# Where a normalised activation starts in SBUF, and how its columns are cut into matmuls, in a fused decoder layer

## The chip, the cores and the metric

The kernel runs on one core of one Trainium2 chip. The metric is the time of one execution on the device in microseconds, the median of several runs. Before the change it is 2046.19 us (three runs, 2044.81 to 2046.81).

## What is computed

One decoder layer with 16 learned meta tokens ahead of 512 positions (L = 528), model width 2048. The first part of the reference is what the change touches:

```python
n = _rmsnorm(h, g_mix[l])
p = n @ w_in[l]
q, k, v, gb, gc, u = jnp.split(p, np.cumsum([...]), axis=-1)
q = _rmsnorm(q.reshape(b, L, N_ATTN_HEADS, HEAD_DIM), g_q[l])
k = _rmsnorm(k.reshape(b, L, N_ATTN_HEADS, HEAD_DIM), g_k[l])
...
o_conv = gb * _causal_dwconv(gc * u, conv_w[l])
```

q, k and v have 8 heads of 128; b, c and u (gb, gc and u above) have 1024 channels. Behind it come the stick-breaking attention, a norm of each group, one output projection with residual, and a SwiGLU feed-forward network (FFN, width 5632) with residual. The meta positions are dropped at the end, so q and b are needed for 512 positions only (META = 16 to L), k and v for all 528.

## The kernel before

Everything is held transposed: channels on the 128 partitions, positions along the free dimension. Products keep float32 accuracy by splitting each operand into a rounded high part and a remainder (type fp32r, 4 bytes) and summing three matmuls: high x high, high x low, low x high (`product_steps`, L311 to L313). The weights arrive by DMA in pieces of 8 k tiles (128 x 1024), ACT writes the high part (L202) and DVE the remainder (L203) into `sw_split`, three buffers deep.

**Normalised x.** `n_tiles` (L353) are 16 tiles, one for each 128 channels, with two rows per partition: row 0 holds the high part (written by ACT, L383), row 1 the low part (DVE, L384). A row is L + 48 floats = 2304 bytes (9 x 256) and a tile 4608 bytes (18 x 256), so all 32 rows start at the same place modulo 256 bytes. In the built program tile n0 starts at byte 104,096 of a partition, which is 160 modulo 256. The data starts 40 floats (160 bytes) into the row, so position 0 lies at 64 modulo 256, position 16 at 128, position 256 at 64.

**The products on n.** Each `product` walks two weight pieces of 8 k tiles. Within a piece it goes over the parts of the output, and within a part over the 8 k tiles, three matmuls each. The parts before the change:

- k and v of each head, 528 positions (`parts_of_all`, L398): 256 positions into the end of one PSUM bank and then 272 into the start of the next. The two lie side by side, and `flat` (L395) reads them as one row of 528.
- q of each head (L416, L530) and the first two b tiles, pb0 and pb1 (L710, L758): 512 positions in one matmul into one bank.
- pc0 and pu0 (L684): two parts of 258 positions from position 14 (C0) on.

The first head's k and q are made together while x arrives (L419 to L433). In the other heads the order is k, q, v. Between matmuls `tick` (L293) calls work that was put off by a number of k tiles (`after`, L290): the norms of k and q, and of the head before, the transposes of v and the scores z (`attend`, L544), the cumulative sums (`sums`, L613) and the weighted sum (`mix`, L643). With one part, `tick` comes after each k tile; with two, after every second step of a part. What TensorE executes is the order that the tile scheduler writes out from this.

**The conv stage.** Pairs of c and u tiles (`conv_pair`, L828, 258 columns) and later of b tiles (`gate_pair`, L840, 256 columns) use a seven-product scheme (`pair_product`, L797, matmuls at L793 to L795). Four of its seven blocks read n itself: `raw_block` from position 14 or 270 (16 or 272 in the gate pairs) and `last_block` (L743), a part of n that eight DMAs (L765) overwrite with mixed data once pb1 has been read; the other three read `mixed` tiles.

**The FFN.** It uses the same `pair_product`, 256 columns at a time, on tiles made by `slots` (L884). There the data starts 4 floats into a tile whose start is 224 modulo 256 bytes, so each operand starts at 240 modulo 256, and all lengths are multiples of 1024 bytes.

The weight operands start at 128 modulo 256 bytes everywhere.

Of the kernel before, what the change touches and what calls it, by code (L numbers as in the profile page):

```python
# [22 lines left out]
KT = D // P  # L23
# [3 lines left out]
T2 = SEQ // 2  # L27
# [6 lines left out]
def hybrid_layer(ctx: ExitStack, tc: tile.TileContext, xT, w_in, w_out, w_gu, w_down, vecs, out):  # L34
# [18 lines left out]
    npool = open_pool("npool", side="right")  # L53
# [21 lines left out]
    g_q, g_k = vec[:, 48:49], vec[:, 49:50]  # L75
# [24 lines left out]
    gq_s = const.tile([P, 1], F32, name="gq_s")  # L100
# [174 lines left out]
    def next_w():  # L275
        ahead = max(min(n_first, used[0] + 6), used[0] + 1 + S_AHEAD)
        if used[0] < n_first:
            ahead = min(ahead, n_first + 1)
        while len(split_w) < min(len(pieces), ahead):
            if n_first < len(split_w) <= n_first + S_AHEAD:  # L280
                with tc.issue_after(read_q0[3].ins):
                    prepare()
            else:
                prepare()
        used[0] += 1
        return split_w[used[0] - 1]
# [3 lines left out]
    def after(k_tiles, work):  # L290
        waiting.append([k_tiles, work])

    def tick():  # L293
        for w in waiting:
            w[0] -= 1
        while any(w[0] <= 0 for w in waiting):
            w = next(w for w in waiting if w[0] <= 0)
            waiting.remove(w)
            w[1]()

    def product_steps(parts, acts, n):

        k, last = 0, n - 1
        while k <= last:

            hi, lo = next_w()
            ws = [(hi[:, a : a + P], lo[:, a : a + P]) for a in range(0, hi.shape[-1], P)]
            for n_part, (ps, a, b) in enumerate(parts):
                for i, (wh, wl) in enumerate(ws):
                    ah, al = acts[k + i]  # L310
                    pe.matmul(ps, wh, ah[:, a:b], start=k + i == 0, stop=False)  # L311
                    pe.matmul(ps, wh, al[:, a:b], start=False, stop=False)  # L312
                    pe.matmul(ps, wl, ah[:, a:b], start=False, stop=k + i == last)  # L313
                    if (n_part * len(ws) + i + 1) % len(parts) == 0:
                        tick()
            k += len(ws)
            yield

    def product(parts, acts):
        for _ in product_steps(parts, acts, len(acts)):  # L320
            pass
# [28 lines left out]


    H = L // 2
    n_tiles = [npool.tile([P, 2, L + 48], F32R, name=f"n{k}")[:, :, 40:] for k in range(KT)]  # L353
    n_parts = [[t[:, part] for part in range(2)] for t in n_tiles]
    npool.tile([P, 52], F32, name="pad_n")
    n_hl = []
# [3 lines left out]
    ms, r, eps_r2, r2 = accs[1], rpool.tile([P, L], F32, name="r"), accs[1], acc  # L360
# [32 lines left out]
            ve.tensor_tensor(accs[k % 2], accs[k % 2], s, ALU.add)  # L393

    def flat(ps):  # L395
        return ps.rearrange("p a b -> p (a b)")[:, T2 : T2 + L]

    def parts_of_all(ps):  # L398
        return [(ps[:, 0, T2:], 0, T2), (ps[:, 1, : L - T2], T2, L)]

    def two(t):
        return t.rearrange("p (a b) -> p a b", a=2)
# [1 line left out]
    def read_qk(ps, g, cols):  # L404

        raw = t512(L, "e", 2)[:, :cols]
        s = t512(L, "e2", 2)[:, :cols]
        sc.activation(s, ps, AF.Square)
        last = sc.activation(raw, ps, AF.Copy, scale=g)
        return raw, s, cols, last  # L410

    pk0 = pp.tile([P, 2, 512], F32, tag="pp", name="pk0")
    pq0 = pp.tile([P, 2, 512], F32, tag="pp", name="pq0")
    steps = [
        product_steps(parts_of_all(pk0), n_hl, KT),
        product_steps([(pq0[:, 0, :], META, L)], n_hl, KT),  # L416
    ]

    for a, b in FIRST:  # L419
# [9 lines left out]
    for a, b in FIRST:  # L429
        for k in range(a, b):  # L430
            split_x(k)
        for step in steps:
            next(step)  # L433
    read_k0, read_q0 = read_qk(flat(pk0), g_k, L), read_qk(pq0[:, 0, :], gq_s, SEQ)
    for k in range(6):
        square_x(k)
    with tc.issue_after(read_k0[3].ins):
# [29 lines left out]
    def load_mix(k):  # L467
        xs[k] = xpool2.tile([P, 4, N], F32, tag="x", name=f"x_mix{k}")
        for m in range(4):
            at = C0 + m % 2 * T2  # L470
            tc.keep_in_program_order(nc.sync.dma_start(xs[k][:, m], xT[k + m // 2 * 8][:, at : at + N]))
# [16 lines left out]
    def qk_norm(read, dst, parts_of, name, then=None):  # L488

        raw, s, cols = read[:3]  # L490
        sh = apool.tile([P, L], F32R, tag="sh", name=f"sh_{name}")[:, :cols]
        sl = apool.tile([P, L], F32R, tag="sl", name=f"sl_{name}")[:, :cols]
        cuts = [(0, cols)] if cols == SEQ else [(0, T2), (T2, L)]
        split(sh, sl, s)

        def finish():
            v = t512(L, "v", 2)[:, :cols]
            for a, b in cuts:
                q = small(f"ss_{name}{a}")[:, : b - a]
                pe.matmul(q, ones_r, sh[:, a:b], start=True, stop=False)  # L500
                pe.matmul(q, ones_r, sl[:, a:b], start=False, stop=True)
                ve.scalar_tensor_tensor(
                    v[:, a:b], q, 1.0 / P, eps_r2[:, L - cols + a : L - cols + b], ALU.mult, ALU.add
                )
            rsqrt(dst, v, cols, times=raw)
            hi, lo, n = parts_of
            last = split(hi, lo, dst[:, :n])
            if then:
                with tc.issue_after(last[0].ins), tc.issue_after(last[1].ins):
                    then()  # L510

        return finish
# [3 lines left out]
    def head(h):  # L516

        if h:
            pk = pp.tile([P, 2, 512], F32, tag="pp", name=f"pk{h}")
            product(parts_of_all(pk), n_hl)  # L520
        read = read_qk(flat(pk), g_k, L) if h else read_k0
        kn = kns[0]
        kh = apool.tile([P, 384], F32R, tag="kh", name=f"kh{h}")
        kl = apool.tile([P, 384], F32R, tag="kl", name=f"kl{h}")
        after(8 if h else 19, qk_norm(read, kn[:, :L], (kh, kl, 384), f"k{h}"))

        if h:
            load_mix(h - 1)
            pq = pp.tile([P, 2, 512], F32, tag="pp", name=f"pq{h}")
            product([(pq[:, 0, :], META, L)], n_hl)  # L530
        read = read_qk(pq[:, 0, :], gq_s, SEQ) if h else read_q0
        qn = apool.tile([P, SEQ], F32, tag="qn", name=f"qn{h}")
        qh = apool.tile([P, SEQ], F32R, tag="qh", name=f"qh{h}")
        ql = apool.tile([P, SEQ], F32R, tag="ql", name=f"ql{h}")
        after(9 if h else 22, qk_norm(read, qn, (qh, ql, SEQ), f"q{h}", (lambda: mix_x(h - 1)) if h else None))

        pv = pp.tile([P, 2, 512], F32, tag="pp", name=f"pv{h}")
        product(parts_of_all(pv), n_hl)
        vt = t512(L, "e", 2)
        with tc.high_priority(0 if h else 1 << 20):  # L540
            ve.tensor_tensor(vt[:, :L], flat(pv), r, ALU.mult)
        after(6 if h else 15, lambda: attend(h, kn, kh, kl, qn, qh, ql, vt))
# [119 lines left out]
    for h in range(HEADS):  # L662
        head(h)
# [43 lines left out]
    y0 = t512(L, "e2", 2)[:, :SEQ]  # L707
    conv3(y0, cu0, 0)
    pb = pp.tile([P, 2, 512], F32, tag="pp", name="pb0")
    product([(pb[:, 0, :], META, L)], n_hl)  # L710
    gb0 = t512(L, "v", 2)[:, :SEQ]
    ve.tensor_tensor(gb0, pb[:, 0, :], r[:, META:], ALU.mult)
    assert not waiting
    apool.release()
    xpool2.release()
# [3 lines left out]
    def oc_slot(i, dt, name):  # L719
        return ocpool.tile([P, SEQ], dt, tag=f"oc{i}", name=name)  # L720
# [34 lines left out]
    CN = SEQ + 2  # L755
    gb1 = oc_slot(7, F32, "gb1")
    pb = pp.tile([P, 2, 512], F32, tag="pp", name="pb1")
    product([(pb[:, 0, :], META, L)], n_hl)  # L758
    ve.tensor_tensor(gb1, pb[:, 0, :], r[:, META:], ALU.mult)
    sm.release()  # L760
    pp.release()
    xyz = open_pool("xyz", 2, space=PSUM)
# [166 lines left out]
    for i, j in enumerate(OUT_TILES):  # L929
# [34 lines left out]
        ps = ps_out[i]  # L964
        half, k = divmod(j, 8)
# [266 lines left out]
```

## Time and profile before

| | |
|---|---|
| median of three runs | 2046.19 us (2044.81 to 2046.81) |
| the profiled execution | 2046.62 us, span 2044.8 us |
| granted TensorE clock | 0.999 of full |
| head stage (first product to the end of v of the last head) | about 6 to 343 us |
| pc0, pu0, pb0, pb1 | 343 to 395 us |
| conv stage | 395 to 600 us |
| output projection | 600 to 774 us |
| FFN | 774 to 2044 us |

TensorE appears as PE (matmuls) and PEld (weight loads), VectorE as DVE, ScalarE as ACT, GpSimd as POOL, SyncE as SP. [...]

A row of the table of windows gives the stretch in us, its length, then for each engine the busy time and the number of instructions, then the granted clock, the busy share of the DMA engines and GB/s. A row of the groups gives line, engine, operation, tiles, shape and count, then busy time and mean ns, then the idle time ahead and what ended it. A row of the timeline gives start, duration, engine, line, operation, tiles and shape, and in brackets a wait ahead of it.

### The profile page before, as it was taken

How to read it: one execution, taken by the hardware profiler on the slowest of the kernel's cores; microseconds unless marked ns; L12 is line 12 of the kernel's file. 1: busy time of each engine (PE TensorE's matmuls, PEld its weight loads, DVE VectorE, ACT ScalarE, POOL GpSimd, SP SyncE). 2: the span in 40 equal slices, each digit the busy share in tenths (PEclk: the TensorE clock that was granted, in tenths of full speed). 3: DMA queues.
4: the chain of work that ended last, by engine and by line, in shares of the span. 5: the costliest groups of instructions: out<-in, count | busy, mean ns of one | idle time of the engine just before them, and what ended most of it. 6: DMA issues, size and time to landing. Idle time of an engine off the chain costs nothing.

```text
span 2044.8 us, 39586 instructions
## 1 busy us (share of the span) xinstructions
PE 2027.8 (99%) x16134; PEld 1962.6 (96%) x16134; DVE 1728.4 (85%) x2187; ACT 1074.9 (53%) x1555; POOL 349.3 (17%) x514
## 2 busy tenths in 40 slices
PE   9999999999999999999999999999999999999999
PEld 8899999899998888999999999999999999999999
DVE  7877677698887778998988988988988978888887
ACT  7766667444454435555555554555555544444443
POOL 0111112200004441011111111111111242131211
PEclk9999999999999999999999999999999999999999
DMA  6343334732355555456465465455455899797764
GB/s 220 105 134 117 122 114 152 268 119 94 114 191 176 172 162 194 142 176 182 138 176 169 133 174 171 136 172 167 141 175 161 271 342 349 171 314 199 214 154 90
DMA packets 156086, 356.28 MB, mean 174 GB/s; under 512 B 13632, under 2 KB 67648, under 8 KB 155136
## 3 DMA queue, kind: packets, MB, share of 16 engines
q1 hardware_dynamic: 72208, 216.76, 32.6%
q0 software_dynamic: 83696, 136.99, 25.0%
q8 instruction: 126, 2.06, 0.4%
q14 instruction: 56, 0.46, 0.1%
HBM read 275.78 MB, written 77.92 MB: 173 GB/s over the span
## 4 chain that ended last, share of the span: by engine, by line
PE 89%; DVE 4%; ACT 2%; DMA 2%; issue 1%; POOL 1%; SPq 0%; DVEq 0%; ACTq 0%
PE x L793 13%; PE x L795 13%; PE x L794 13%; PE z L794 6%; PE z L795 6%; PE z L793 6%; PE y L795 3%; PE y L793 3%; PE y L794 3%; DVE sw_split L203 2%; PE pv L311 1%; PE pv L312 1%; PE pv L313 1%; PE pq L313 1%; PE pq L312 1%
## 5 line engine op out<-in xcount | busy, mean ns | idle before, releaser
L202 ACT CAST sw_split<-sw_in 128x1024 fp32r<-128x1024 f32 (+2 forms) x668 | 661.5, 992 | 712.1 <-PE z L794 189.0
L203 DVE TENSOR_TENSOR sw_split<-sw_in,sw_split 128x1024 fp32r<-128x1024 f32 (+2 forms) x668 | 778.0, 1165 | 150.2 <-ACT sw_split L202 144.7
L793 PE MATMUL x<-f,sw_split 128*128 128x256 f32 x1408 | 388.3, 276 | 2.9 <-ACT sides L813 1.9
L795 PE MATMUL x<-f,sw_split 128*128 128x256 f32 x1408 | 388.2, 276 | 0.6 <-DVE sw_split L203 0.6
L794 PE MATMUL x<-f,sw_split 128*128 128x256 f32 x1408 | 388.1, 276 | 0.0
L793 PEld LDWEIGHTS x<-f,sw_split 128*128 128x128 f32 x1408 | 265.0, 188 | 3.3 <-ACT sides L813 2.1
L795 PEld LDWEIGHTS x<-f,sw_split 128*128 128x128 f32 x1408 | 265.1, 188 | 1.0 <-DVE sw_split L203 1.0
L794 PEld LDWEIGHTS x<-f,sw_split 128*128 128x128 f32 x1408 | 265.1, 188 | 0.0
L1047 POOL DMA_DIRECT2D fd<-s x147 | 103.7, 922 | 713.7 <-DVE s L324 713.0
L209 DVE TENSOR_TENSOR sw_in<-sw_in 128x1024 f32<-128x1024 f32 (+1 forms) x164 | 187.9, 1146 | 11.5 <-DMA sw_in<-w_in 3.0
L793 PE MATMUL z<-f,sw_split 128*128 128x256 f32 x704 | 193.7, 275 | 0.3 <-ACT sides L815 0.3
L794 PE MATMUL z<-f,sw_split 128*128 128x256 f32 x704 | 193.6, 275 | 0.0
L795 PE MATMUL z<-f,sw_split 128*128 128x256 f32 x704 | 193.6, 275 | 0.0
L795 PE MATMUL x<-ring,sw_split 128*128 128x256 f32 x608 | 167.3, 275 | 0.4 <-DVE sw_split L203 0.4
L793 PE MATMUL x<-ring,sw_split 128*128 128x256 f32 x608 | 167.2, 275 | 0.0
L794 PE MATMUL x<-ring,sw_split 128*128 128x256 f32 x608 | 167.2, 275 | 0.0
L793 PEld LDWEIGHTS z<-f,sw_split 128*128 128x128 f32 x704 | 132.2, 188 | 0.5 <-ACT sides L815 0.5
L794 PEld LDWEIGHTS z<-f,sw_split 128*128 128x128 f32 x704 | 132.2, 188 | 0.0
L795 PEld LDWEIGHTS z<-f,sw_split 128*128 128x128 f32 x704 | 132.2, 188 | 0.0
L795 PEld LDWEIGHTS x<-ring,sw_split 128*128 128x128 f32 x608 | 114.1, 188 | 0.6 <-DVE sw_split L203 0.6
L794 PEld LDWEIGHTS x<-ring,sw_split 128*128 128x128 f32 x608 | 114.1, 188 | 0.0
L793 PEld LDWEIGHTS x<-ring,sw_split 128*128 128x128 f32 x608 | 114.1, 188 | 0.0
(604 smaller groups left out, 5459.2 us busy)
## 6 DMA issues: line engine op xcount, KB each, us to landing
sw_in<-w_gu SPq DMA_DIRECT2D x176, 512.0 KB, 3.9
sw_in<-w_in SPq DMA_DIRECT2D x92, 512.0 KB, 3.3
fd<-s POOLq DMA_DIRECT2D x147, 256.0 KB, 5.3
sw_in<-w_down SPq DMA_DIRECT2D x96, 384.0 KB, 4.2
ring<-fd POOLq DMA_DIRECT2D x42, 768.0 KB, 16.8
sw_in<-w_out SPq DMA_DIRECT2D x32, 512.0 KB, 3.4
out_T<-d POOLq DMA_DIRECT2D x54, 256.0 KB, 5.2
mix_dram<-st_x POOLq DMA_DIRECT2D x16, 516.0 KB, 4.0
```

Source lines behind the costliest of these rows:

```text
L202: sc.copy(hi, src)
L203: ve.tensor_tensor(lo, src, hi.bitcast(F32), ALU.subtract)
L209: return ve.tensor_tensor(sums[name], a, b, ALU.add)
L311: pe.matmul(ps, wh, ah[:, a:b], start=k + i == 0, stop=False)
L312: pe.matmul(ps, wh, al[:, a:b], start=False, stop=False)
L313: pe.matmul(ps, wl, ah[:, a:b], start=False, stop=k + i == last)
L793: pe.matmul(p, hi[:, kk], ah, start=start and j == k == 0, stop=False, skip_group_check=skip)
L794: pe.matmul(p, hi[:, kk], al, start=False, stop=False, skip_group_check=skip)
L795: pe.matmul(p, lo[:, kk], ah, start=False, stop=k == n - 1, skip_group_check=skip)
L1047: gp.dma_start(fd[c][s][:, :, k], t[:, :, i])
```

## The change

The data of n starts 4 floats into the row instead of 40; tile sizes and all other places are the same. Position 0 then lies at 176 modulo 256 bytes, positions 16 and 272 at 240. k and v are cut as 272 and then 256 positions instead of 256 and then 272. q and the two plain b tiles become two matmuls of 256 positions, the first into the second half of one bank, the second into the first half of the next, and are read across the two.

```diff
-    n_tiles = [npool.tile([P, 2, L + 48], F32R, name=f"n{k}")[:, :, 40:] for k in range(KT)]
+    n_tiles = [npool.tile([P, 2, L + 48], F32R, name=f"n{k}")[:, :, 4:] for k in range(KT)]
...
     def flat(ps):
-        return ps.rearrange("p a b -> p (a b)")[:, T2 : T2 + L]
+        return ps.rearrange("p a b -> p (a b)")[:, SEQ - META - T2 : SEQ + T2]
 
     def parts_of_all(ps):
-        return [(ps[:, 0, T2:], 0, T2), (ps[:, 1, : L - T2], T2, L)]
+        return [(ps[:, 0, SEQ - META - T2 :], 0, META + T2), (ps[:, 1, :T2], META + T2, L)]
+
+    def parts_of_seq(ps):
+        return [(ps[:, 0, T2:], META, META + T2), (ps[:, 1, :T2], META + T2, L)]
+
+    def flat_seq(ps):
+        return ps.rearrange("p a b -> p (a b)")[:, T2 : T2 + SEQ]
...
-        product_steps([(pq0[:, 0, :], META, L)], n_hl, KT),
+        product_steps(parts_of_seq(pq0), n_hl, KT),
...
-    read_k0, read_q0 = read_qk(flat(pk0), g_k, L), read_qk(pq0[:, 0, :], gq_s, SEQ)
+    read_k0, read_q0 = read_qk(flat(pk0), g_k, L), read_qk(flat_seq(pq0), gq_s, SEQ)
...
-            product([(pq[:, 0, :], META, L)], n_hl)
-        read = read_qk(pq[:, 0, :], gq_s, SEQ) if h else read_q0
+            product(parts_of_seq(pq), n_hl)
+        read = read_qk(flat_seq(pq), gq_s, SEQ) if h else read_q0
...
-    product([(pb[:, 0, :], META, L)], n_hl)
+    product(parts_of_seq(pb), n_hl)
...
-    ve.tensor_tensor(gb0, pb[:, 0, :], r[:, META:], ALU.mult)
+    ve.tensor_tensor(gb0, flat_seq(pb), r[:, META:], ALU.mult)
...
-    ve.tensor_tensor(gb1, pb[:, 0, :], r[:, META:], ALU.mult)
+    ve.tensor_tensor(gb1, flat_seq(pb), r[:, META:], ALU.mult)
```

The conv stage's code is not edited, but its blocks on n move with the tile: starts of 120 modulo 256 become 232, and 128 becomes 240 (258 columns); in the gate pairs 128 becomes 240, and 136 becomes 248 (256 columns).

More of the change, by code (lines that the diff above doesn't have):

```diff
@@ L757, in hybrid_layer @@
     pb = pp.tile([P, 2, 512], F32, tag="pp", name="pb1")
-    product([(pb[:, 0, :], META, L)], n_hl)
-    ve.tensor_tensor(gb1, pb[:, 0, :], r[:, META:], ALU.mult)
+    product(parts_of_seq(pb), n_hl)
+    ve.tensor_tensor(gb1, flat_seq(pb), r[:, META:], ALU.mult)
     sm.release()
```

## The prediction

> **What bounds the kernel now.** I read the page first (parts 1 and 4: who is busy, what the last chain is made of), then the table of windows, then the groups of matmuls by form, and then the timeline at the matmuls that the change touches.
>
> ```profile
> PE 2027.8 (99%) x16134; PEld 1962.6 (96%) x16134; DVE 1728.4 (85%) x2187; ACT 1074.9 (53%) x1555; POOL 349.3 (17%) x514
> ...
> PE 89%; DVE 4%; ACT 2%; DMA 2%; issue 1%; POOL 1%; SPq 0%; DVEq 0%; ACTq 0%
> ```
> ```profile
> 0.00:10.00 10.00, 8.32 (x38) 6.86 (x38) 4.13 (x13) 5.71 (x11) 1.09 (x8) 1.00 0.75 225
> 10.00:20.00 10.00, 9.80 (x58) 8.13 (x58) 9.81 (x16) 10.00 (x19) 0.00 (x0) 1.00 1.05 391
> ...
> 200.00:300.00 100.00, 99.13 (x683) 92.17 (x683) 71.67 (x119) 65.53 (x110) 14.95 (x35) 1.00 0.36 117
> ```
>
> TensorE is the end of the chain nearly everywhere; in the head stage (200 to 300 us) it is busy for 99.13 of 100 us, with DVE at 72% and ACT at 66%. So the time is the number of matmuls times their spacing, plus a few waits. A matmul's duration overlaps the next one's, so I use the distance from start to start, which the page does not print. The timeline does:
>
> ```profile
> 328.43 0.28 PE L311 MATMUL pv<-n,sw_split 128*128 128x256 f32 x1
> ...
> 331.25 0.29 PE L311 MATMUL pv<-n,sw_split 128*128 128x272 f32 x1
> ...
> 334.22 0.28 PE L311 MATMUL pv<-n,sw_split 128*128 128x256 f32 x1
> ```
> ```profile
> 323.83 0.40 PE L311 MATMUL pq<-n,sw_split 128*128 128x512 f32 x1
> ...
> 327.96 0.39 PE L623 MATMUL c<-sph,carry 128*128 128x512 f32 x1
> ```
> ```profile
> 384.19 0.39 PE L311 MATMUL pb<-n,sw_split 128*128 128x512 f32 x1
> ...
> 395.07 0.40 PE L673 MATMUL ss_a<-acc_hi,ones_r 128*128 128x512 f32 x1
> ```
> ```profile
> 459.41 0.28 PE L793 MATMUL x<-n,sw_split 128*128 128x256 f32 x1
> ...
> 462.28 0.28 PE L793 MATMUL z<-mixed,sw_split 128*128 128x256 f32 x1
> ```
> ```profile
> 470.87 0.28 PE L793 MATMUL x<-n,sw_split 128*128 128x256 f32 x1
> ...
> 473.67 0.27 PE L793 MATMUL y<-n,sw_split 128*128 128x256 f32 x1
> ```
> ```profile
> 799.87 0.28 PE L793 MATMUL z<-f,sw_split 128*128 128x256 f32 x1
> ...
> 801.91 0.28 PE L793 MATMUL z<-f,sw_split 128*128 128x256 f32 x1
> ```
>
> From the first row of a stretch to the first row behind it, divided by the matmuls between:
> - v's 256-wide part, 24 matmuls: 2.82/24 = 117.5 ns. Its 272-wide part, 24: 2.97/24 = 123.8 ns.
> - q, 512 wide, 18: 4.13/18 = 229.4 ns; the second plain b tile, 48: 10.88/48 = 226.7 ns.
> - conv stage, 256 wide on n: 2.87/24 = 119.6 ns in one block and 2.80/24 = 116.7 ns in another of the same pair.
> - FFN, 256 wide on its own tiles, 18: 2.04/18 = 113.3 ns.
>
> The same 256 columns thus cost 113.3, 116.7, 117.5 or 119.6 ns. What differs, by the built program's layout, is where the moving operand starts modulo 256 bytes: 240 in the FFN, 64 for v, 128 and 136 in the two conv blocks, which read the same tiles 8 bytes apart. The weights are at 128 in all of them. Before the change n starts at 64; afterwards at 176, so that its position 16 (where q starts) and its position 272 both lie at 240, the FFN's place.
>
> **The change, part by part.** Counts follow from the loops (16 k tiles, 3 matmuls each, per product; 8 k tiles per block), and the groups of matmuls agree; each row is one of the three lines:
>
> ```profile
> L311 PE MATMUL pq<-n,sw_split 128*128 128x512 f32 x128 | 50.3, 393 | 0.0
> ...
> L793 PE MATMUL x<-n,sw_split 128*128 128x258 f32 x168 | 47.6, 283 | 1.0 <-ACT sw_split L202 1.0
> ```
>
> 1. *k and v, 256-wide part*, now at 240: 16 products x 16 x 3 = 768 matmuls from 117.5 to the FFN's 113.3, **-3.2 us**. Bounds: 0 (rate of the stage) and -3.2.
> 2. *k and v, 272-wide part*, now at 176, a start that no wide row shows. At the FFN's rate it would take 113.3 x 272/256 = 120.4 ns, at today's 123.8; upwards, the same surcharge as between the FFN and the worse conv block (6.3 ns) gives 126.7. I take 122, the middle of the first two, since its end falls at 240: 768 x 1.8 = **-1.4 us**, ends -2.6 and +2.2.
> 3. *q and plain b in two parts at 240*: 8 and 2 products, 384 + 96 matmuls of 229.4 and 226.7 become 960 of 113.3, 226.6 a pair. Not every q stretch is as slow as the quoted one, so I take 2 ns for q and nothing for b: **-0.8 us**, ends 0 and -1.1 (all of q at 229.4); upwards, the first rival.
> 4. *Conv stage, 256 wide*: three of the four blocks on n move from 128 to 240: 3 gate pairs x 3 blocks x 24 = 216 matmuls from 119.6 to 113.3, **-1.4 us**. The fourth (72) goes from 136 to 248; by the nearest rows 113.3 to 119.6, I take no change.
> 5. *Conv stage and first c and u tiles, 258 wide*: starts of 120 become 232 (168 x 3 in the pairs, 192 in pc0 and pu0), and 128 becomes 240 for 168. No row shows 258 columns at these starts: I take zero for the 696, with the ends of this view:
>
> ```profile
> 366.02 0.28 PE L311 MATMUL pu<-n,sw_split 128*128 128x258 f32 x1
> ...
> 370.31 0.39 PE L623 MATMUL c<-sph,carry 128*128 128x512 f32 x1
> ```
>    36 matmuls in 4.29 us are 119.2 ns; at the FFN's rate 258 columns are 114.2, so the lower end is 696 x 5.0 = -3.5 us; the same 5.0 the other way is +3.5. For the 168 at 240 I take 2 ns, **-0.3 us**.
>
> The items sum to -7.1 us. [...]
>
> What is given back. Inside a head, TensorE waits for a chain that it does not speed up:
>
> ```profile
> 305.84 0.29 PE L311 MATMUL pk<-n,sw_split 128*128 128x272 f32 x1
> 306.20 0.46 PE L563 MATMUL z<-qh,kh 128*128 128x400 f32 x1
> ```
> ```profile
> 317.97 0.29 PE L620 MATMUL c<-bh,ones_r 128*128 128x288 f32 x1
> 318.62 0.40 PE L621 MATMUL c<-bl,ones_r 128*128 128x288 f32 x1 [0.36 <-DVE bl L324]
> ```
>
> From the second z (it waits for the copies of the transposed v to free its PSUM buffer; the k matmul in between ends that wait partly, and the scheduler now puts it behind z instead) to bl, ACT, DVE and POOL set the pace. Between the two quoted pairs stand 12 matmuls of k's second part, 24 + 24 of its next block and the first 12 of q: the first 12 turn from 272 wide to 256 at 240, so the change takes 12 x 10.5 + 24 x 4.2 + 24 x 1.8 ns = 0.27 us out of this stretch. TensorE would come to bl that much earlier and wait for it: 7 heads x 0.27 = **+1.9 us**; the other end is 0, if bl too comes earlier because ACT and DVE take the segments in another order.
>
> Behind the waiting matmul stands the rest of q, and nothing but TensorE waits for that. The first head's k, 48 x 6.0 = 0.3 us, I count as lost: in the first 20 us TensorE starts 96 matmuls only and DMA is at 0.75 to 1.05, so x and the weights set the pace. **+0.3 us**.
>
> Costed at nothing: ACT and DVE now read q and b from two PSUM banks instead of one. They do so for k already:
>
> ```profile
> L408 ACT ACTIVATE tmp<-pk x8: 598/600/610, 28.4 to 317.6; 128x528 f32<-128x528 f32 x8
> L408 ACT ACTIVATE tmp<-pq x8: 567/592/595, 31.7 to 329.3; 128x512 f32<-128x512 f32 x8
> ```
> 600 ns for 528 columns against 592 for 512 leaves no extra, and ACT at 66% hides it; uncovered it would be some 10 ns a head. The 480 extra weight loads of q and b lie under matmuls, as in the FFN, which loads weights for every 256 columns at 113.3 ns. The hooks that place the attention's steps between matmuls fire at the same distances: after every k tile of q before, after every second half-long step now. ACT and DVE write n at other addresses with the same shapes. The eight transfers into n (L765) still wait for the second b tile, whose parts are both read within each block of eight, so a block ends where it ended; SP's and POOL's queues issue the same transfers.
>
> Sum: -7.1 + 2.2 = **-4.9 us**. From the profiled execution's 2046.62 us (its span is 2044.8, with 1.8 around it) that is 2041.7; the median of the runs shown, 2046.19, is 0.4 lower, so I forecast **2041.3 us**.
>
> **The rivals.**
> - *Slower: 256 columns on n stay at the rate of the stage.* If the FFN's 113.3 belongs to its tiles (long runs, hi and lo 8 KB apart; in n they are 2304 bytes apart) and 256-wide reads of positions 16 on keep the conv stage's 119.6, q pays 384 x (239.2 - 228.6) and b 96 x (239.2 - 226.7), together +5.3 us, items 1, 2 and 4 give nothing, and z's second matmuls, held up by a k matmul of 0.12 us that now comes behind them, add 5 heads x 0.12: 2046.19 + 5.9 = 2052.1. It decides from 114.3 ns for a half of q, above which the split costs. For it: only the FFN shows 113.3. Against it: 116.7 and 119.6 in the same tiles 8 bytes apart. Chance 0.12. [...]
> - *The gain is made and waited away.* If all of items 1 and 2 (4.6) ends in waits inside the heads and only items 3 to 5 stay: 2046.19 - 2.5 = 2043.7. For it: the 0.36 us wait for bl stands in the head already. Against it: only 60 of the 192 matmuls of k and v in a head lie between z and bl. Chance 0.18.
> - *All reads of n reach the FFN's rate.* Then item 2 gives 1.2 more, the 696 of item 5 give 3.5 and its 168 another 0.5: 5.2 us more than forecast, 2036.1. For it: 232 and 176 are near 240. Against it: 258 columns have never been below 119 in a quoted stretch. Chance 0.15.
>
> **How the numbers follow.** Forecast 0.55, rivals 0.12, 0.18 and 0.15. The forecast's own range is 2038 to 2044.5 (items 2 and 5 by half of their ends). Leaving out the slower case and a few per cent at either end, the range is 2035.8 to 2046.5. A measurement tells about 0.2% (4.1 us) from no change, so faster is below 2042.1: two thirds of the forecast case (0.37) and the last rival, 0.52. Slower is above 2050.3: 0.12. The rest is 0.36.
>
> **What would show it.** Right: 24 matmuls of k's or v's second part in 2.72 us; a pair of q's halves in 227 ns; 272 columns between 120.4 and 123.8; conv stretches of 24 in 2.72 us instead of 2.87; the wait for bl longer by up to 0.3 us a head; the FFN unchanged. Wrong: q's halves at 117 or more each; 272 columns above 124; 258 columns off 119 by more than 2 ns; a new wait on L765 or on the weight splits in the first conv pair.

## The result, and the profile after

The changed kernel took 2049.93 us (median of 17 runs, 2046.09 to 2052.31), the kernel before on the same chip 2044.88 (17 runs, 2044.19 to 2047.72). The ratio is 1.0020, with a 95% interval of 1.0012 to 1.0027: slower by about 4 us, where 2041.3 us and a gain of 4.9 were forecast. The time lies above the range (2046.5).

The page of the changed kernel, parts 1 and 4:

```profile
PE 2026.5 (99%) x16614; PEld 1981.9 (97%) x16614; DVE 1725.4 (84%) x2187; ACT 1075.0 (53%) x1555; POOL 343.8 (17%) x514
...
PE 89%; DVE 4%; ACT 3%; issue 2%; DMA 1%; POOL 1%; SPq 0%; DVEq 0%; ACTq 0%
```

The bound is what it was: TensorE, with 480 matmuls more. Its head stage in the table of windows:

```profile
200.00:300.00 100.00, 98.65 (x780) 95.59 (x779) 70.23 (x119) 64.96 (x109) 13.25 (x35) 1.00 0.36 117
```

98.65 us busy instead of 99.13: a little more waiting. The rates are read from the timeline, as before, from the first row of a stretch to the first row behind it. v of the last head (24 matmuls of 272 columns, then 24 of 256):

```profile
328.99 0.29 PE L311 MATMUL pv<-n,sw_split 128*128 128x272 f32 x1
...
332.03 0.28 PE L311 MATMUL pv<-n,sw_split 128*128 128x256 f32 x1
...
334.75 0.29 PE L311 MATMUL pv<-n,sw_split 128*128 128x272 f32 x1
```

272 columns at 176: 3.04/24 = 126.7 ns in this stretch and 125.5 in the mean over all of k and v, not 122 (before: 123.8 in the quoted stretch, 123.6 in the mean). 256 columns at 240: 2.72/24 = 113.3, as forecast, but not in every stretch: the mean over all 768 is 114.5. Why shows in q of the same head:

```profile
315.20 0.28 PE L311 MATMUL pq<-n,sw_split 128*128 128x256 f32 x1
...
317.92 0.36 PE L624 MATMUL c<-sph,later_r 128*128 128x432 f32 x1
...
319.13 0.40 PE L627 MATMUL c<-bl,ones_r 128*128 128x288 f32 x1 [0.52 <-DVE bl L324]
319.37 0.28 PE L311 MATMUL pq<-n,sw_split 128*128 128x256 f32 x1
...
320.78 0.28 PE L311 MATMUL pq<-n,sw_split 128*128 128x256 f32 x1
...
322.14 0.28 PE L506 MATMUL ss_k<-sh_k,ones_r 128*128 128x256 f32 x1
```

Ahead of the c matmuls, 24 halves take 2.72 us (113.3 ns). Behind them the same halves, with the same tiles and places, take 1.41/12 = 117.5 ns for the first 12, and 1.36/12 = 113.3 for the next 12. Behind these matmuls of the attention the rate takes some 12 matmuls to settle again (117.5 ns, then 113.3), and in a head there are such breaks all the time. v shows it too: the 256-wide part quoted above has 113.3 ns from its first matmul on, but v's last one (at 340.59 us), ahead of which matmuls of the attention break into the 272-wide part, takes 118.1 ns for 12 matmuls and 113.3 for the next 12. The wait for bl is 0.52 us instead of 0.36. In the conv stage (24 matmuls from the first row of each pair to the second):

```profile
441.00 0.29 PE L799 MATMUL x<-n,sw_split 128*128 128x258 f32 x1
...
443.95 0.28 PE L799 MATMUL z<-mixed,sw_split 128*128 128x258 f32 x1
...
452.57 0.28 PE L799 MATMUL x<-n,sw_split 128*128 128x258 f32 x1
...
455.41 0.28 PE L799 MATMUL y<-n,sw_split 128*128 128x258 f32 x1
...
461.31 0.28 PE L799 MATMUL x<-n,sw_split 128*128 128x256 f32 x1
...
464.08 0.28 PE L799 MATMUL z<-mixed,sw_split 128*128 128x256 f32 x1
...
472.61 0.29 PE L799 MATMUL x<-n,sw_split 128*128 128x256 f32 x1
...
475.52 0.28 PE L799 MATMUL y<-n,sw_split 128*128 128x256 f32 x1
```

258 columns at 232 take 2.95/24 = 122.9 ns (119.2 before, at 120), at 240 118.3; 256 columns at 240 take 115.4 (119.6 before), at 248 121.3 (116.7 before, at 136). One wait there became longer, that of TensorE for the low part of split weights in the first conv pair; before (PE at L795), then after, with the operations of DVE that lead to it:

```profile
410.81 1.22 DVE L209 TENSOR_TENSOR sw_in<-sw_in 128x1024 f32<-128x1024 f32 x1 [2.86 <-DMA sw_in<-w_in]
411.95 1.22 DVE L203 TENSOR_TENSOR sw_split<-sw_in,sw_split 128x1024 fp32r<-128x1024 f32 x1
413.23 0.39 PE L795 MATMUL x<-n,sw_split 128*128 128x258 f32 x1 [1.70 <-DVE sw_split L203]
```
```profile
412.20 1.23 DVE L209 TENSOR_TENSOR sw_in<-sw_in 128x1024 f32<-128x1024 f32 x1 [3.56 <-DMA sw_in<-w_in]
413.34 1.22 DVE L203 TENSOR_TENSOR sw_split<-sw_in,sw_split 128x1024 fp32r<-128x1024 f32 x1
414.62 0.39 PE L801 MATMUL x<-n,sw_split 128*128 128x258 f32 x1 [2.40 <-DVE sw_split L203]
```

The wait is 2.40 us instead of 1.70. DVE makes that low part behind a sum of weights (L209), and the sum waits for a weight transfer to land.

**Where the time went.** First starts of the product tiles, in the timelines of the two profiled executions, mark off the stages:

| stage | before, us | after, us | difference |
|---|---|---|---|
| heads (first k to pc0) | 336.70 | 337.72 | +1.02 |
| pc0, pu0, pb0, pb1 | 52.45 | 52.60 | +0.15 |
| conv stage (y0 to the first po) | 204.45 | 205.70 | +1.25 |
| output projection (to the first y) | 174.63 | 174.62 | 0 |

So ahead of the output projection 2.4 us are more work or waiting. The rest has to do with the granted clock, the share of TensorE's full clock that the profile shows as granted. The profile before has one stretch of 3.4 us at half clock, in the FFN (at 804.9 us), which costs about 1.7 us (an estimate, half of its length); the profile after happens to have none there. From its first matmul to its last the FFN takes 1265.9 us before and 1263.5 after; beside the 1.7 that is 0.7 us less, in waits further on. So the span after is no longer than before (2044.4 against 2044.8 us). These figures of one pair of profiles hold to about 1 us only: in a second profile of the kernel before (e1_before) the first head alone is 0.7 us shorter (36.4 against 37.1). Each run also lists its mean granted clock. Where that is 1.000, the changed kernel took 2046.8 us (3 runs), where it is 0.998, 2050.9 (7 runs). The 3.1 us between a median run and those at 1.000 are, at the estimated 1.7 us each, one or two such stretches.

### The profile page after: what moved, and what is told of

Same layout as the page of the kernel before. It is cut to its first block, busy times and chain, and to the rows that moved or that the text cites. A ratio compares the mean times of both kernels' runs of the same rounds, so it can differ in the third digit from the quotient of the medians.

```text
span 2044.4 us, 40554 instructions
## 1 busy us (share of the span) xinstructions
PE 2026.5 (99%) x16614; PEld 1981.9 (97%) x16614; DVE 1725.4 (84%) x2187; ACT 1075.0 (53%) x1555; POOL 343.8 (17%) x514
## 4 chain that ended last, share of the span: by engine, by line
PE 89%; DVE 4%; ACT 3%; issue 2%; DMA 1%; POOL 1%; SPq 0%; DVEq 0%; ACTq 0%
PE x L799 13%; PE x L801 13%; PE x L800 13%; PE z L799 6%; PE z L800 6%; PE z L801 6%; PE y L799 3%; PE y L800 3%; PE y L801 3%; PE pv L311 2%; PE pv L313 2%; PE pv L312 2%; DVE sw_split L203 1%; PE pq L312 1%; PE pq L313 1%
## 5 line engine op out<-in xcount | busy, mean ns | idle before, releaser
L209 DVE TENSOR_TENSOR sw_in<-sw_in 128x1024 f32<-128x1024 f32 (+1 forms) x164 | 187.9, 1146 | 10.4 <-DMA sw_in<-w_in 4.0
```

The source lines that it names most:

```text
L209: return ve.tensor_tensor(sums[name], a, b, ALU.add)
```

## The experiments

Each kernel computes all of the reference, save three that only run stretches of matmuls (e2_sweep, e3_sweep, e4_history). Ratios are against the kernel before in the same job.

### Repeats: is it real?

Both kernels unchanged (e1_after, e1_before), and the changed one again in a later job (e3_after).

> The changed kernel once more, for a second profile and for the granted clock of each run. Theory 'dips': the loss of 5 us is about 1.2 us of work (TensorE reached the output projection 1.9 us later, 0.7 of it not in the rates) and 3 to 4 us of stretches of 3.4 us in which half the clock is granted, each worth 1.7 us; so runs with a mean clock of 1.000 take 2046 to 2047, and each 0.001 below costs 2 us, and a profile at 0.998 or 0.999 shows one or two such stretches ahead of 830 us, right behind a wait of TensorE. Rival 'rates': the slow runs have slower matmuls at the full clock; then a slow run shows no stretch at half clock and other spacings on n.

> The kernel before, once more, as its own control. 'Dips': 2044.8 without a stretch at half clock (mean clock 1.000), 2046.6 with one, and fewer than one on average. 'Rates': the same time at any mean clock.

> The changed kernel once more, in the job of the start tests. Theory of two parts (2.3 us more work at full clock, and the rest in more half-clock stretches): ratio 1.0015 to 1.0022; runs that list a clock of 1.000 are 2 to 2.5 us above those of the kernel before that do; the profile's output projection begins 1.9 to 2.4 us later than before, counted from the first matmul, and if it holds two stretches at half clock, the second stands behind the waits at the start of the FFN or behind the 2.6 us wait in the first conv pair. Rival (the excess is measurement of one job): ratio 1.0010 or less.

Measured: 1.0017 (1.0008 to 1.0026), 1.0000 (0.9992 to 1.0009) and again 1.0017 (1.0008 to 1.0026). The loss is real, about 3.5 us in these jobs. In the new profiles of the changed kernel the output projection begins 2.9 and 3.9 us later than in the first profile of the kernel before, counted from the first product; the second has a half-clock stretch at 9.1 us, while x still arrives, and its first head takes 1.4 us longer than in the first profile of the changed kernel. The time goes with the granted clock, as the theory of the dips had it, but its split was wrong: among runs that list 1.000 the changed kernel is 2.5 us (one run against 13) and 3.1 us (three against 8) slower than the kernel before, so most of the loss is there at full clock, where the theory had 1.2 us. Of e3_after's expectation the ratio came; its later start of the output projection (1.9 to 2.4 us) and its difference at full clock (2 to 2.5) were too small.

### The start alone, the cuts alone

e1_start_only is the kernel before with n at 176; e1_parts_only has all new cuts, with n at 64 as before.

```diff
-    n_tiles = [npool.tile([P, 2, L + 48], F32R, name=f"n{k}")[:, :, 40:] for k in range(KT)]
+    n_tiles = [npool.tile([P, 2, L + 48], F32R, name=f"n{k}")[:, :, 4:] for k in range(KT)]
```

> Only the start of n moves (4 floats into the row); k and v stay 256 then 272, q and b stay whole. By the rates of the profile after: conv and c, u at 232 +2.0 us, 256-wide gate blocks -0.8, k and v with all parts at 176 +1 to +3, q and b at 240 unknown, 0 to +4. Time without dips 2046 to 2052. If the dips come from the start of n (a later conv stage), the mean clock falls as in the changed kernel; if they come from the split of q and b, it stays as before.

> Only the cuts change; n stays where it was, so q's and b's halves lie at 128, k's and v's second part at 128, the first at 64. If the start decides the rate, halves at 128 cost the 119.6 ns of the conv stage: q and b +5, k and v second part +1.6, conv unchanged: 2051 without dips. If the start does not matter: 2045 to 2046. Dips as in the changed kernel if the split of b brings them, as before if the start does.

Measured: 1.0014 (1.0005 to 1.0022) and 1.0036 (1.0023 to 1.0048). Each half loses by itself. The start alone leaves the clock where it was (0.55 thousandths below 1, the kernel before 0.56); the cuts alone took 2050.6 us in their one run at 1.000, where 2051 was expected if the start decides. Mean start-to-start distances in the two timelines:

| columns | before | start alone | cuts alone | both |
|---|---|---|---|---|
| k, v: 256 | 117.6 at 64 | 118.4 at 176 | 119.6 at 128 | 114.5 at 240 |
| k, v: 272 | 123.6 at 64 | 125.0 at 176 | 123.9 at 64 | 125.5 at 176 |
| q: 512, or two of 256 | 228.7 at 128 | 230.9 at 240 | 239.0 at 128 | 229.6 at 240 |
| conv: 258 | 119.2 at 120 | 122.9 at 232 | 119.2 at 120 | 122.6 at 232 |

The same start gives nearly the same rate in either kernel; the cut matters through the starts that it makes. With the cuts, two more things come: the scheduler puts no k matmul ahead of the second z any more, and the wait in the first conv pair is 2.44 us (before: 1.70).

### One part left out

e2_kv_only keeps the start and k's and v's cuts, with q and b whole; e2_b_whole leaves only the plain b tiles whole:

```diff
-    product(parts_of_seq(pb), n_hl)
+    product([(pb[:, 0, :], META, L)], n_hl)
...
-    ve.tensor_tensor(gb0, flat_seq(pb), r[:, META:], ALU.mult)
+    ve.tensor_tensor(gb0, pb[:, 0, :], r[:, META:], ALU.mult)
...
```

> The changed kernel with q and b whole: n starts at 176, k and v are 272 then 256. By the profiles' rates q and b at 240 cost 1.3 ns more per 512 columns than two halves at 240: +0.5 for q. If the cuts of k and v bring the new order of z (0.3 us a head more around z), that stays; if the halves of q do, it goes, 2.4 us in all. So 2048 to 2049 in the first case and about 2046.5 in the second.

> The changed kernel with the two plain b tiles whole again (512 columns at 240). The wait of TensorE for split weights in the first conv pair was 2.6 us after the change and in the parts-only kernel, and 1.5 to 1.9 with whole b. If the halves of b cause it, it falls back by 0.7 to 1.1 us, and the time with it (less 0.2 for the rate). If the extra half-clock stretches come from that wait, the mean clock rises from 0.9987 to 0.9994 as well, and the median falls by 2 us in all; if not, by 0.7.

Measured: 1.0004 (0.9995 to 1.0013) and 1.0010 (1.0001 to 1.0019). With b whole the conv wait falls from 2.40 us to 1.50 and the conv stage from 205.70 to 204.95: b's halves cause it. The mean clock of e2_b_whole is back at that of the kernel before in its job (0.7 thousandths short, both). The profiles of all full kernels agree. Counted from the first matmul of the conv stage, the weight transfer that L209 waits for lands at 16.1 to 16.4 us in the seven with b in halves and at 15.2 to 15.7 in the eight with b whole, though it is issued at 8.2 to 8.4 us in each. In both kernels here the heads stay at 170.9 us from the first k of head 3 to that of head 7, counted from 0 (before 170.24, after 170.76), and no k matmul stands ahead of the second z. So neither q's nor b's halves cause that loss; it stays with k's and v's cuts and the new start together. For e2_kv_only 2048 to 2049 us was expected in this case; it took 2047.0, with 2046.4 for the kernel before in its job, so less than expected is lost. Its ratio and that of e2_b_whole lie within each other's intervals.

### A table of starts

e2_sweep runs stretches of 24 matmuls on one tile at rising starts; e3_sweep does that for 256 columns four times, with the weights' place, the direction, and the other engines' work changed.

> Leaves out the whole layer: it copies one x tile and one weight tile into SBUF and times matmuls alone, 24 at a time as in a product (high x high, high x low, low x high over 8 k tiles), for 32 starts of the moving operand, 8 bytes apart modulo 256, at 256, 258, 272 and 512 columns, and at 256 columns once more with the weights at 0 instead of 128 modulo 256. Nothing else runs. Theory 'start decides': at 256 columns 113.3 ns at 240, about 117.6 at 64, 118.4 at 176, 119.6 at 128, 116.8 at 136, 121.3 at 248; 272 columns 123.6 at 64 and 125.3 at 176; 258 columns 119.2 at 120 and 122.5 at 232; 512 columns 227.5 at 128 and 229.6 at 240. If what counts is the distance from the weights, the map moves by 128 bytes with them. Rival 'the stage decides': every start costs the same when nothing else runs.

> Only a sweep; the kernel's work is left out. 256 columns at the 32 starts, four times: weights at 128 modulo 512, at 384 as in the kernel, again in the other direction, and again with DVE and ACT at work beside; hi and lo 2304 bytes apart as in n. Theory (start modulo 256 decides, the rest not): four equal tables, 114.2 ns at 64 and 116.4 at 240. Rival A (the weights' place modulo 512 or the distance of hi and lo matters): tables one to three show the kernel's 117.6 at 64, 116.8 at 136 and 114.4 at 240 from the second on. Rival B (traffic of the other engines matters): only the fourth shows these.

Some of the ns per matmul, each from the first row of its stretch to the next one's (beside them the mean rates in the kernels that have that start; 256 columns at 8 and 258 at 64 are from e3_start_8, below):

```
start      256 rising   256 falling   kernel's 256    258 rising   kernel's 258
    8         120.1        122.2          121.7          118.5          -
   64         114.2        117.8          117.6          121.0        120.7
  120         119.7        120.0            -            119.1        119.2
  128         119.7        119.2          119.6          119.8        120.0
  136         120.0        116.8          116.8          118.7          -
  176         118.3        118.5          118.4          119.5          -
  232         120.0        119.6            -            122.4        122.6
  240         116.4        115.4          114.5          118.8        118.6
  248         120.6        121.5          121.3          117.8          -
```

The rate jumps from one multiple of 8 to the next (256 rising: 120.0, 116.4 and 120.6 at 232, 240 and 248); no neighbour tells of it. 272 columns range from 123.3 (48) to 128.6 (8), with 126.7 at 176; 512 from 227.5 at 128 (the place of q before) to 239.8 at 248. Three values that were expected of e2_sweep from the kernels did not come: 117.6 at 64 (measured 114.2), 116.8 at 136 (120.0) and 113.3 at 240 (116.4). With weights at 0 instead of 128, the table moves by 128 (114.2 then at 192; 30 of 31 starts within 0.2 ns): the distance between the two operands counts. In e3_sweep, weights 256 bytes further, and DVE and ACT at work beside, changed nothing (within 0.3 ns): rivals A and B fall. But the falling direction gave other values at 8, 64 and 136, and these are the kernel's. The theory of e3_sweep, four equal tables, fell too.

### What stood before

e4_history runs only stretches of 24 at five starts, each twice, behind six others.

> Only stretches of 24 matmuls; the kernel's work is left out. 256 columns at 64, 136, 240, 8 and 128 (weights at 384 as in the kernel), each twice in a row, behind a stretch at 56, 72, 0, 128, 176 or 240, and at the end behind 512 columns. Theory (besides the start, the phase that the stretch before leaves behind decides): the same start takes two or more values, by what stood before: 114.2 or 117.8 at 64, 120.0 or 116.8 at 136, 116.4, 115.4 or 114.4 at 240, and the second stretch stays near the value of the first. Rival (the second sweep's other values belong to its falling order of addresses alone): each start has one value behind all six, that of the rising sweep, save behind 72 (64) where it falls.

The first row of each stretch at 64 (psb, psc), behind 56 and then behind 72 (psa); the last row is the next psa:

```profile
32.74 0.28 PE L54 MATMUL psa<-big,wtb 128*128 128x256 f32 x1
...
35.62 0.28 PE L54 MATMUL psb<-big,wtb 128*128 128x256 f32 x1
...
38.37 0.28 PE L54 MATMUL psc<-big,wtb 128*128 128x256 f32 x1
...
41.08 0.28 PE L54 MATMUL psa<-big,wtb 128*128 128x256 f32 x1
...
43.97 0.28 PE L54 MATMUL psb<-big,wtb 128*128 128x256 f32 x1
...
46.79 0.28 PE L54 MATMUL psc<-big,wtb 128*128 128x256 f32 x1
...
49.62 0.28 PE L54 MATMUL psa<-big,wtb 128*128 128x256 f32 x1
```

Behind 56 the second stretch at 64 takes 2.71/24 = 112.9 ns (113.3 before rounding to 0.01 us), behind 72 2.83/24 = 117.9. The whole run: 64 stays at 117.8 behind 72 and behind 512 columns, and goes to 113.3 behind 0, 56, 128, 176 and 240. 136 stays at 120.0 behind 56, 72, 128, 240 and 512, and at 116.7 behind 0 and 176. 8 stays at 122.7 behind 56 and 128, else at 120.0. 240 takes 114.9 to 115.8 in its first stretch behind any other and 113.3 in every second one; 128 has 119.5 to 120.0 throughout. So each of these five starts has one or two lasting rates, what stood before picks one, and it is not reached at once. The rival (one value a start, save for the direction) falls. For the prediction this matters: 113.3 ns is not the mark of 240 alone. 64, where n started before, has it too, but behind what stands there in the kernel it keeps 117.8.

### Blind tests of the table

The kernel before, nothing changed but n's start: 240 (`[:, :, 20:]`) and 8 (`[:, :, 26:]`). Cuts and orders stay as they were.

> The kernel before with one number changed: n starts at 240 modulo 256 instead of 64, no cut changed, so the order on every engine stays as it was. Theory (the start of the moving operand modulo 256, against weights at 128, sets each group's spacing, and the first sweep's table holds in the kernel too): k and v 256 wide (240) 114.4 ns instead of 117.6, 272 wide (240) 123.4 instead of 123.6, q and b 512 wide (48) 233.1 instead of 228.5, conv 258 wide (40 and 48) 120.1 instead of 119.2, gate 256 wide (48, 56) 119 to 120; sum of the rates -2.6 + 2.2 + 0.7 = +0.3 us, so the ratio lies within 0.9990 and 1.0010. Rival (240 is simply the good place, as the prediction had it): q and b do not get slower, and the ratio is 0.9985 or less.

> The kernel before with n at 8 modulo 256 and nothing else, a start that no kernel has had: the sweep's table has 256 columns at 120.1 ns and 272 at 128.6 there, 512 at 72 at 233.3, 258 at 64 and 72 at 121.0 and 121.3. Theory (the table holds in the kernel): k and v +5.8 us, q and b +2.3, conv stage +1.7, together +9.8 us: ratio 1.0048, between 1.003 and 1.006. Rival (the table belongs to matmuls with nothing beside them, and any start other than 64 costs what 176 cost, 3 us): ratio 1.0014.

Measured: 1.0005 (0.9996 to 1.0015) and 1.0037 (1.0024 to 1.0049). v in e3_start_8, stretches of 24:

```profile
332.37 0.28 PE L311 MATMUL pv<-n,sw_split 128*128 128x256 f32 x1
...
335.31 0.29 PE L311 MATMUL pv<-n,sw_split 128*128 128x272 f32 x1
...
338.39 0.29 PE L311 MATMUL pv<-n,sw_split 128*128 128x256 f32 x1
```

122.5 and 128.3 ns, where the table has 120.1 rising (on which the expectation rested), 122.2 falling, and 128.6: for one number in one line, 7.6 us between the medians. Both ratios lie in the theory's ranges, and both rivals fall. The 7.6 us are less than the 9.8 of the rates for a reason that the trace shows: with slower matmuls TensorE waits less inside the heads. Its idle time ahead of the bl matmuls adds up to 0.3 us (2.1 in the kernel before), ahead of z's first matmuls to 0.1 (0.6). At 240, q and b rose to 232.7 and 232.5 (table 233.1), k's and v's 256 columns fell to 115.6 and 116.3 only, 272 came to 124.4 (table 123.4), conv's 258 to 119.9 (table 120.1).

### The order of z, and the parts added up

e4_swap computes k's and v's 256-wide part first, which puts a k matmul back ahead of the second z; e4_swap_b_whole has b whole besides; e4_b_parts is the kernel before with b alone in halves.

```diff
-        return [(ps[:, 0, SEQ - META - T2 :], 0, META + T2), (ps[:, 1, :T2], META + T2, L)]
+        return [(ps[:, 1, :T2], META + T2, L), (ps[:, 0, SEQ - META - T2 :], 0, META + T2)]
```

> The changed kernel with k's and v's parts in the other order (256 positions at 240 first, then 272 at 176), which puts a k matmul back between the first and the second z, as in the kernel before. Theory (the heads' loss of 0.13 us each comes from z, which waits since that k matmul stands behind it): the z matmuls of four heads take 8.8 us instead of 10.0, and the stretch from the first k of head 3 to that of head 7 falls from 170.8 to 170.3 or less; kernel 0.9 us shorter than the changed one, ratio 1.0013 where that has 1.0017. Rival (the wait moves to bl or to the k matmuls behind z, since ACT and DVE set the pace there): 170.7 to 170.9, ratio 1.0017.

> The same with the plain b tiles whole (512 wide at 240), which keeps the conv stage's first wait at 1.7 us instead of 2.6. Theory (heads, conv wait and half-clock stretches add up): 0.9 + 0.75 us less than the changed kernel at full clock and a clock shortfall of 0.6 to 0.8 instead of 1.2 thousandths: ratio 1.0005, between 1.0000 and 1.0010; what is left is the 258-wide conv blocks at 232 (+1.7 us) against the gate pairs (-0.8 us). Rival (the parts of the loss overlap, so that less comes back): ratio 1.0012.

> The kernel before with the plain b tiles alone in two halves (at 128, where 256 columns take 119.6 ns): 96 matmuls of 227.4 become pairs of 239.2, +1.1 us. Theory (b's halves lengthen the first conv pair's wait for the low weights from 1.9 to 2.6 us): another +0.7 us, ratio 1.0009. If that wait is also what brings the changed kernel's additional half-clock stretches, the mean shortfall of the granted clock rises from 0.6 to about 1.1 thousandths and the ratio is 1.0014; rival for this: it stays at 0.6.

Measured: 1.0017 (1.0008 to 1.0026), 1.0008 (0.9999 to 1.0017) and 1.0008 (1.0000 to 1.0017). In e4_swap the z matmuls of four heads went from 10.02 us back to 8.76, but the four heads only from 170.76 to 170.50 (before 170.24), and the ratio did not fall. The timeline of after, then of e4_swap, shows what stays:

```profile
305.50 0.47 PE L569 MATMUL z<-qh,kh 128*128 128x512 f32 x1
...
306.59 0.45 PE L569 MATMUL z<-qh,kh 128*128 128x400 f32 x1 [0.16 <-DVE v L561]
```
```profile
305.92 0.47 PE L569 MATMUL z<-qh,kh 128*128 128x512 f32 x1
...
306.70 0.29 PE L311 MATMUL pk<-n,sw_split 128*128 128x272 f32 x1
307.14 0.45 PE L569 MATMUL z<-qh,kh 128*128 128x400 f32 x1 [0.15 <-DVE v L561]
```

From the first z to the second it is 1.09 us without a k matmul between and 1.22 with one: DVE's copies release the second z at their own time. The order accounts for half of the heads' loss (0.26 of 0.52 us). The other half fits the pace of ACT and DVE, for which TensorE waits there, but no run isolates it; neither the theory (170.3 or less) nor the rival (170.7 to 170.9) hit the stretch. With b whole too, 1.0008 lies midway between the theory (1.0005) and the rival (1.0012), and its interval holds both, so whether the parts of the loss simply add up stays open. In e4_b_parts b took 1.2 us more and the conv stage 0.74, as the theory had it.

e4_swap's profile also caught what no earlier one had: a half-clock stretch in the conv stage. Its wait in the timeline, and the table of windows (columns: stretch, length, PE, PEld, DVE, ACT and POOL busy, granted clock, DMA share, GB/s):

```profile
412.42 0.28 PE L801 MATMUL z<-mixed,sw_split 128*128 128x258 f32 x1
415.07 0.39 PE L801 MATMUL x<-n,sw_split 128*128 128x258 f32 x1 [2.38 <-DVE sw_split L203]
```
```profile
411.00:415.50 4.50, 2.12 (x18) 1.92 (x17) 2.81 (x3) 1.04 (x1) 0.00 (x0) 1.00 0.48 117
415.50:418.90 3.40, 3.40 (x18) 3.40 (x17) 2.25 (x3) 0.00 (x0) 0.00 (x0) 0.50 0.40 145
418.90:425.00 6.10, 6.10 (x51) 5.98 (x51) 4.61 (x7) 2.68 (x3) 0.00 (x0) 1.00 0.32 91
```

0.4 us behind the end of the wait of 2.4 us the clock falls to 0.50 for 3.4 us, and TensorE starts 18 matmuls there instead of some 28. Over all runs with b in halves (74, of seven kernels: the changed one thrice, e1_parts_only, e4_swap, e4_b_parts and e2_fill, described below), the mean clock falls short of 1 by 1.1 thousandths (0.8 to 1.35 by kernel); in the kernel before, 99 runs of four jobs, by 0.7; in the six other kernels with b whole by 0.4 to 0.7. 0.4 thousandths of 2046 us are 0.8 us. e4_b_parts alone (0.9 against 0.8 in its job) doesn't show the difference, and of the seven profiles with that wait at some 2.4 us or more only this one has the stretch. So its share in the loss rests on the pooled runs and the one stretch that was caught.

### Filling the FFN's wait

Other such stretches stand at the start of the FFN, behind waits of 1.8 to 1.9 us in its first two pairs (the kernel before: a wait of 1.90 us, then a granted clock of 0.51 over 804.8 to 808.3 us). e2_fill puts 14 and 28 small matmuls, whose results nothing uses, into these waits.

```diff
+    def fill(n):
+        for m in range(n):
+            tc.keep_in_program_order(pe.matmul(spare[:, :P], ones_r, ones_r, start=True, stop=True))
...
+        if i == CONV + 1:
+            fill(28)
...
+            if i == CONV:
+                fill(14)
```

> The changed kernel with 14 and 28 matmuls of 128 columns, ones times ones into a spare PSUM bank, put where TensorE waits 0.7 to 2 us in the first two gate pairs of the FFN. They add no work to the layer's result. If the half-clock stretches come from those waits, all runs show a clock of 1.000 and the time is that of the changed kernel without them, 2046.8, some 2 us below its median; if the extra ones come from the wait in the first conv pair, the mean clock stays below 1.000 by about 0.0007 and 1 us or less is gained; if the stretches have another cause, nothing changes.

Measured: 1.0028 (1.0017 to 1.0038), a miss. From the first y of the first pair to that of the second it is 40.94 us (after, without a half-clock stretch: 38.37). The 28 took the place of a wait of 1.9 us but last 3.07 us; behind the 14, TensorE still waits 0.9 us for DVE. Seven of the eight runs still list 0.999, so runs fall short of full clock without the 1.9 us wait too; where in the span, these runs don't show.

No kernel of the study is faster than the one before; the first sweep's table, with the kernels' own rates where known, has no start that gives a smaller sum than 64 with the old cuts (144 comes within 0.2 us).

## Why the prediction was wrong

| step of the prediction | forecast, us | measured, us |
|---|---|---|
| 1: k, v, 256 wide, at 240 | -3.2 | -2.4 |
| 2: k, v, 272 wide, at 176 | -1.4 | +1.5 |
| 3: q and b in halves | -0.8 | +0.4 |
| 4: gate pairs, 256 wide | -1.4 | -0.8 |
| 5: 258 wide | -0.3 | +1.8 |
| sum of the rates | -7.1 | +0.5 |
| given back in the heads | +2.2 | +1.6 |
| first conv pair's wait | 0 | +0.7 |

The measured column is counts by the change of the mean distances; the heads' +1.6 is their +1.02 less the rates in them (-2.4, +1.5 and +0.3). The rows add up to +2.8, the stages to +2.4; the -0.4 between them was not taken apart. Most of the miss is the sum of the rates: 7.6 us.

- **The premise** (the start modulo 256 sets the rate) was right in the main, and it holds blind: e3_start_8. It was incomplete: the four prices were read as four starts, but 64 and 136 have two lasting rates each (e4_history), so that part of what was read as the place was what stood before.
- **Step 1, "to the FFN's 113.3"**, failed in part. 113.3 is the settled rate. Parts of k and v that nothing breaks reach it; where matmuls of the attention break in, the first 12 or so behind them take up to 118.1, and the mean is 114.5.
- **Step 2, "I take 122"**, failed, with 125.5 measured and its bound of 126.7 at hand; at 2.9 us it is the largest single miss. The middle of two rates at other starts is no estimate where the rate jumps from one multiple of 8 to the next.
- **Step 3** failed by the same settling. b, 48 in a row at one start, does reach 113.9 a half; q, broken by the attention's matmuls, 114.8: 229.6 a pair against 228.7, a loss of 0.4 us, beyond the rival's decision point of 114.3.
- **Step 4** was right in kind; 248 gave +0.3 where nothing was taken.
- **Step 5, "zero for the 696"**, is the next in size (2.1 us off): the 696 cost +2.0 of the +3.5 allowed above. 258 columns at 232 take 122.6 ns in the conv stage, not 119.2. A known bound was taken as balanced when only a run at 232 could tell.
- **What is given back** was right in place and near in size (+2.2, measured +1.6; the wait for bl +0.16 in the quoted head). TensorE's idle time in the two traces says the same without the rates: ahead of the bl matmuls it adds up to 2.1 us before and 3.1 after, ahead of z's first matmuls to 0.6 and 1.1, together +1.5. That these waits nearly vanish in e3_start_8 shows it from the other side. The second z waits for DVE's copies, as said there.
- **"A block ends where it ended"**, of the transfers into n and the b halves, was argued and wrong: the wait for the weight splits in the first conv pair, listed among the signs of failure, rose by 0.7 us. e2_b_whole and e4_b_parts show that the halves do it, and the traces that the last link is a weight transfer which lands 0.7 us later. Why it takes longer, no run isolates.
- **No step spoke of the clock.** By the pooled runs another 0.8 us or so is half-clock stretches, one of them caught behind that very wait. With the 2.4 us of the stages that makes 3.2 of the 3.5 us (1.0017), but the agreement is rough, since single profiles differ by 1 us and the FFN gave 0.7 back in the quoted pair.

The rival "256 columns on n stay at the rate of the stage" gave a time near the measured one (2052.1) by luck, for a reason that isn't so: 256 columns did leave that rate, by 3 to 7 ns at 240. What held of it is its decision point, 114.3 ns for a half of q, and its term for the second z, 0.6 us (idle time there: +0.5).

## What to carry to other kernels

Where TensorE is the bound, measure the spacing at the very start, width and predecessor that the new kernel has; a rate seen at another place, or in a long run, is no price (256 columns at 240: 113.3 ns in the FFN, 114.5 in k and v). Moving a tile moves every read of it, so the widths that nobody meant to change need a row of their own in the sum. A wait of 2 us on TensorE can cost more than its length: behind 9 of the 24 waits of 1.7 us or more in these profiles the clock was at half for 3.4 us, about 1.7 us lost by the estimate above.

## What the runs showed of the hardware

- 256 columns on full 128x128 weights cost 113.3 to 122.7 ns by the start of the moving operand modulo 256 bytes relative to the weights (e2_sweep, e3_sweep, e4_history), and 512 cost 226.7 (b in the kernel before) to 239.8 (at 248 in e2_sweep). With the weights at 0 instead of 128 the table of starts moved by 128 bytes (114.2 ns at 192 instead of 64). Weights 256 bytes further, and work of DVE and ACT beside, changed nothing (within 0.3 ns).
- Some starts have two lasting rates (64: 113.3 and 117.8; 136: 116.7 and 120.0; 8: 120.0 and 122.7), picked by the matmuls that ran before (e4_history). Why, no run here tells.
- In the profiles of the full kernels, half clock came, ahead of the last matmul, in ten stretches of 3.41 us: nine behind a single wait of 1.8 to 2.4 us, one at 9.1 us, while x arrives, behind three waits of 1.0 us together. The granted clock was 0.50 over the 3.4 us in e4_swap (415.5 to 418.9 us) and 0.51 over 804.8 to 808.3 us in the kernel before.
